# Routing from the residual's own rows: norm weights into the router's rows, norms into the logits

## The chip, the cores and the metric

One Trainium2 chip, of which the program uses one core. The metric is the device time of one launch in microseconds (us). The kernel before took 1364.86 us, the median of three runs (1364.3, 1364.86 and 1366.51 us).

## The reference

The reference is a decoder trunk of two layers on 256 tokens of width 1024, in float32. Layer 0 is a Conformer convolution beside cross-attention to a memory, then a dense SwiGLU. Layer 1 is a sliding-window attention beside cross-attention, then a mixture of eight experts of width 3584, of which each token takes two. What the change touches is the way from the end of layer 1's attention to the experts:

```
h  = h + swa_mixer(rms_norm(h, sw_attn_norm_g), ...)    # ends with concat([o, m]) @ w_out
hn = rms_norm(h, sw_ffn_norm_g)                         # h * rsqrt(mean(h*h) + eps) * g
logits = hn @ router                                    # 256 x 8
top_v, top_i = top_k(logits, 2); top_w = softmax(top_v)
h = h + sum_e gate_e * (silu(hn @ we_gate[e]) * (hn @ we_up[e])) @ we_down[e]
```

The logits are a sum over the channels of h, the norm's weight g and the router's row, times one number for each token, the root of the mean square.

## The kernel before

The kernel is written for a planner that places each engine's instructions in the order in which a timeline of its own finds them ready, earlier lines of the program first among the ready; it sets the semaphores itself. Each engine then runs its list in order, and so does SP, which issues nearly all loads. Inside the experts' loop TensorE's order is the written one (`manual_schedule`, L1026). A tile that is laid on bytes of an older tile waits until the older tile's last reader is done (`reuse_waits="tile"`).

Layer 1's attention writes its queries, transposed, into `q1T` (six blocks of 128 channels by 256 tokens, 1 KB a partition each, L582), the memory's queries into `mq1T` and the keys into `kTs`. The scores (L251) read them. The output projection (`project_out`, L308) goes over two halves n of the output's channels. In each half two accumulators, one for each 128 tokens t, take 24 products of 128x512 each (each float32 weight is split into a high and a low part, `mm3`). Then `add_residual` (L300) adds the accumulator to h, and takes the sum of squares for the norm; after the second half `token_rstd` gives rs2[t], the norm of each token.

The second part of the function opens new pools in the place of the first part's. `gain` (L673) is the norm's weight g, copied to all 128 partitions by one load of 512 KB (L674) on SP, and scaled by GpSimd (L675). After it SP issues the first 19 units of the experts' weights (L725), most of them 896 KB or 1 MB, each into a slot that the layers before leave free: two of the slots are those of layer 1's normed input, eight those of split weights, two those of the projection's input. `hn` (L756) is h times rs2 times `gain`, on VectorE. TensorE transposes hn block by block (L766), the copies go to `xT` (L767), and 16 matmuls against the router's rows (L770), each on 32 columns of the array, give partial logits `plt`. A copy (`lt`, L773) and four small matmuls (L776) add them up with tokens on partitions, and L778 copies the logits `lg`. From there a chain of small VectorE instructions finds the two best experts, counts the places with matmuls by triangular ones (L796 to L800), clears the accumulators `po` and `py` (L831, L833), and builds the selection matrices `Pm` of the first expert (L896). `gather` (L901) multiplies blocks of hn by Pm (32 matmuls, L909), which gives the first expert's tokens `xe`. Then the loop over 32 rounds (eight experts by four blocks of 896) begins: `gate_up` (L926), the same for a busy expert's further tokens (`gate_up_over`, L934, in four of the experts here), `down` (L982). After each round SP fetches the units of a later one into the slots that TensorE has read (`fetch`, L1062).

The small norm weights come in as rows through `param_rows` (L118, L368), are transposed at L401 and scaled at L403 to L406. In the new pools, `one` holds `lg`, `hn` and the small tiles, `mwk` the selection matrices, and `rt` holds `gain`, `router`, `xT` and `lt`. `wk`, `big` and `big1` are pools of the first part.

Of the kernel before, what the change touches and what calls it, by code (L numbers as in the profile page):

```python
# [7 lines left out]
F32 = mybir.dt.float32  # L8
# [5 lines left out]
OP = mybir.AluOpType  # L14
# [3 lines left out]
P = 128  # L18
S = 256
D = 1024  # L20
KD = D // P
# [3 lines left out]
HD = 64  # L25
FF = 2816
NE = 8
# [20 lines left out]
def hybrid_kernel(  # L48
# [7 lines left out]
    act, dve, pool, pe, sp = nc.scalar, nc.vector, nc.gpsimd, nc.tensor, nc.sync  # L56

    consts = ctx.enter_context(tc.tile_pool(name="consts", bufs=1))
# [44 lines left out]
    h = consts.tile([P, 2, D], F32, name="h")  # L103
# [3 lines left out]
    ident = consts.tile([P, P], F32, name="ident")  # L107
# [8 lines left out]
    offs = {}  # L116
# [16 lines left out]
    n0 = param_rows(rows0, (("cvg", cv_attn_norm_g, D), ("bglu", cv_b_glu, 2 * CH)), 0, first)  # L133
    for dst, src in first:
        sp.dma_start(dst, src)
    cols = consts.tile([P, P], F32, name="cols")
# [30 lines left out]
    with ExitStack() as ph:  # L167
# [5 lines left out]
        def bank(tag, name):  # L173

            if tag in ("mm", "tp"):
                return psb.tile([P, 512], F32, name=name, tag=tag)
            return psx[-1].tile([P, 512], F32, name=name, tag=tag,
                                bufs=dict(sc=2, cv=1, o=1, acc=4, so=1)[tag])
# [64 lines left out]
        big1 = None  # L243
# [56 lines left out]
        def add_residual(ps, t, n, ssum):  # L300
            hs = h[:, t, n * 512:(n + 1) * 512]
            dve.tensor_tensor(hs, ps, hs, op=OP.add)
            if n == 0:
                first_sum(ssum, t, hs, junk_tile())
            else:
                return token_rstd(ssum, t, hs, junk_tile())

        def project_out(unit, cT, order):  # L308

            ssum = new_sums()  # L310
            for n in range(2):
                acc = [bank("mm", f"wo{t}") for t in range(2)]
                w = []
                for i, t in ((0, 0), (0, 1), (1, 0), (1, 1)) if n == 0 else ((0, 0), (1, 0), (0, 1), (1, 1)):
                    if len(w) == i:
                        w.append(unit(n, i))
                    for j in range(4):
                        mm3(acc[t], [c[:, order[4 * i + j], t * P:(t + 1) * P] for c in cT],
                            [c[:, j, :] for c in w[i]], i == 0 and j == 0, i == 1 and j == 3)
                rs = [add_residual(acc[t], t, n, ssum) for t in range(2)]  # L320
            return rs


# [23 lines left out]
        eye4 = consts.tile([P, 32], F32, name="eye4")  # L347
# [15 lines left out]
        small = []  # L363
        for q in range(GT):
# [4 lines left out]
                                ("lnb", cv_ln_b, CH), ("hmk", mem_k_norm_g, HD), ("hmq0", cv_memq_norm_g, HD),  # L369
                                ("ffg", cv_ffn_norm_g, D), ("swg", sw_attn_norm_g, D),  # L370
                                ("hsq", sw_q_norm_g, HD), ("hsk", sw_k_norm_g, HD),
                                ("hmq1", sw_memq_norm_g, HD)), n0, small)
        for i in range(1, 3):
            for o in (0, CH):
                for dst, src in small[:5]:
# [25 lines left out]
        pe.transpose(pc[:, :n1 - n0], rows1[:n1 - n0, :], ident[:n1 - n0, :n1 - n0])  # L401
        dve.tensor_copy(cols[:, n0:n1], pc[:, :n1 - n0])
        for name, n, f in (("memg", KD, 32.0), ("ffg", KD, 32.0), ("swg", KD, 32.0),  # L403
                           ("hmk", 1, 8.0), ("hsk", 1, 8.0)):
            c = cols[:, offs[name]:offs[name] + n]
            dve.tensor_scalar_mul(c, c, f)  # L406

# [3 lines left out]
        router0 = consts.tile([P, KD, NE], F32, name="router0")  # L411
# [43 lines left out]
        for c in range(NCT):  # L455
# [8 lines left out]
            for g in range(GT):  # L464
                for q in range(4):
                    pe.matmul(pcv[q * 32:(q + 1) * 32, :], T[:, g, q, :], sh[q][:, 4 * g:4 * g + S],
                              start=(g == 0), stop=(g == GT - 1), tile_position=(0, q * 32))
# [104 lines left out]
        c1 = pair_tile("d")  # L572
# [79 lines left out]
                part(1, 1, 0, 3)  # L652
            return halves(t)

        rs2 = project_out(unit1, c1, wo_order)

# [2 lines left out]
    with ExitStack() as ph:  # L661
# [84 lines left out]
                           channel_multiplier=-1)  # L746
        onesb = one.tile([P, P], BF16, name="onesb")
        pool.memset(onesb, 1.0)
        router = rt.tile([P, KD, 32], F32, name="router")
        pool.memset(router, 0.0)  # L750
        pool.tensor_copy(router[:, :, 0:NE], router0)


        hn = one.tile([P, 2, D], F32, name="hn")
        for t in range(2):
            dve.scalar_tensor_tensor(hn[:, t, :], h[:, t, :], rs2[t][:, 0:1], gain, op0=OP.mult, op1=OP.mult)  # L756


        xT = rt.tile([P, KD, S], F32, name="xT")
        plt = bank("plt")[:, :S]  # L760
        for kk in range(KD // 2):
            b = prt.tile([P, 512], F32, name="rtb", tag="gu").rearrange("p (a n) -> p a n", a=2)
            for t in range(2):
                for a in range(2):
                    k = 2 * kk + a
                    pe.transpose(b[:, a, t * P:(t + 1) * P], hn[:, t, k * P:(k + 1) * P], ident)  # L766
            (act.copy if kk % 2 else dve.tensor_copy)(xT[:, 2 * kk:2 * kk + 2, :], b)  # L767
            for k in range(2 * kk, 2 * kk + 2):
                q = k % 4
                pe.matmul(plt[q * 32:(q + 1) * 32, :], router[:, k, :], xT[:, k, :], start=(k < 4), stop=(k >= 4),  # L770
                          tile_position=(0, q * 32))
        lt = rt.tile([P, S], F32, name="lt")
        act.copy(lt, plt)  # L773
        pl = bank("pl")
        for t in range(2):
            pe.matmul(pl[:, t * NE:(t + 1) * NE], lt[:, t * P:(t + 1) * P], eye4[:, 0:NE], start=True, stop=True)  # L776
        lg = one.tile([P, 2, NE], F32, name="lg")
        dve.tensor_copy(lg, pl[:, :2 * NE].rearrange("p (t e) -> p t e", t=2))  # L778
        mx = one.tile([P, 2, 8], F32, name="mx")
        ix = one.tile([P, 2, 8], U32, name="ix")  # L780
        ixf = one.tile([P, 2, 2], F32, name="ixf")
# [47 lines left out]
        py = [fixed(f"py{n}") for n in range(2)]  # L829

        dve.memset(po, 0.0)  # L831
        for n in range(2):
            dve.memset(py[n], 0.0)  # L833

        def gates():

# [53 lines left out]
        def places(e):  # L890

            pos = posm if e == 0 else posm2
            Pm = [wk.tile([P, 2, P], F32, name=f"Pm{n}", tag=f"Pm{n}", bufs=1) for n in range(2)]
            for n in range(2):
                for t in range(2):
                    dve.tensor_scalar(Pm[n][:, t, :], rows2[n], pos[:, t, e:e + 1], None, op0=OP.is_equal)  # L896
            return Pm
# [3 lines left out]
        def gather(e, Pm):  # L901

            xe = wk.tile([P, KD, SL], F32, name="xe", tag="xe")
            for kk in range(2):
                b = bank("ga")[:, :4 * SL].rearrange("p (k n) -> p k n", k=4)
                for a in range(4):
                    k = kk * 4 + a
                    for t in range(2):
                        pe.matmul(b[:, a, :], hn[:, t, k * P:(k + 1) * P], Pm[0][:, t, :SL], start=(t == 0),  # L909
                                  stop=(t == 1))  # L910
                (act.copy if kk else dve.tensor_copy)(xe[:, kk * 4:kk * 4 + 4, :], b)
            b = bank("pmt")
            for n in range(2):
                for t in range(2):
                    pe.transpose(b[:, n * S + t * P:n * S + (t + 1) * P], Pm[n][:, t, :], ident)
            PT = wk.tile([P, 2, S], F32R, name="PT", tag="PT")
            act.copy(PT, b.rearrange("p (n s) -> p n s", n=2))
            return xe, PT
# [106 lines left out]

        with tc.manual_schedule(engines={mybir.EngineType.PE}):  # L1026
            xe = {0: gather(0, places(0))}
            turns_of()
            gates()
            permuted(G2, G)  # L1030
            prev = None
            ys = None
            flag = None
            for i in range(len(rounds) + 1):
                last_round = i == len(rounds)
                if not last_round:
                    e, p = rounds[i]
                    wgu = [ahead.pop(0) for _ in range(8)]
                    if p == NR - 1 and e + 1 < NE:
                        Pm = places(e + 1)  # L1040
                    gate_up(xe[e][0], wgu, range(4))
                if prev is not None:
                    wd = [ahead.pop(0) for _ in range(4)]
                    hT, hTo = hidden_T(*prev[2:])
                if ys is not None:
                    scatter(*ys)
                    ys = None
                if not last_round:
                    if p == NR - 1 and e + 1 < NE:
                        xe[e + 1] = gather(e + 1, Pm)  # L1050
                    over_parts((e, xe[e][0], wgu, range(4)), None)
                    gate_up(xe[e][0], wgu, range(4, KD))
                    hx = hidden()
                over_parts(None if last_round else (e, xe[e][0], wgu, range(4, KD)),
                           None if prev is None else (prev[0], prev[1], hTo, wd))
                if prev is not None:
                    down(prev[1], hT, wd)
                    if prev[1] == NR - 1:
                        ys = (prev[0], outputs(), xe[prev[0]][1])
                if not last_round:  # L1060
                    prev = (e, p, hx, hidden_over())
                    fetch(8 + 4 * (i > 0))  # L1062
            scatter(*ys)
# [107 lines left out]
```

## Time and profile before

| | |
|---|---|
| median of three runs | 1364.86 us |
| the profiled execution's own time | 1362.78 us |
| its span, first to last instruction | 1361.1 us |
| TensorE matmul busy | 1286.2 us (94%) |
| VectorE, ScalarE, GpSimd busy | 387.5, 298.7, 70.7 us |
| mean granted TensorE clock | 0.980 of full speed |
| bytes moved | 420.87 MB, mean 309 GB/s |

The busy times are sums over the whole span; a matmul that waits in the array counts as busy, so 94% doesn't say that TensorE is what limits. The layers before the experts take the first 489 us, the experts the rest. A time in the rows below is counted from the first instruction.

### The profile page before, as it was taken

Reading aid. Unit: us, or ns where it says so; the run is one execution under the profiler, and the core shown is the slowest. Engines: PE = TensorE matmul, PEld = TensorE weight load, DVE = VectorE, ACT = ScalarE, POOL = GpSimd, SP = SyncE. Lnnn points to the kernel's source line nnn. Section 1 sums busy time; section 2 is a strip of 40 time slices with the busy share of each in tenths; the row PEclk is TensorE's granted clock in tenths of the full one; section 3 lists DMA queues with packets and bytes.
Section 4 is the critical chain, followed back from the end, with each engine's and each line's share of the span. In section 5 each row is a group of like instructions: output and inputs, shape, how many; then the busy total and the mean of one; then the engine's idle time right before and its main releaser. Section 6 shows DMA issues by size and latency. Waiting matters only on the chain. (4 is left out here: it accounts for less than half of the span.)

```text
span 1361.1 us, 19725 instructions
## 1 busy us (share of the span) xinstructions
PE 1286.2 (94%) x7908; PEld 720.4 (53%) x7908; DVE 387.5 (28%) x782; ACT 298.7 (22%) x575; POOL 70.7 (5%) x110
## 2 busy tenths in 40 slices
PE   6978799999898879999999999999999999999997
PEld 5844589999775643344454343444343454434443
DVE  5633465555466421012112111111110211100212
ACT  6333354444365300001111000011000111000111
POOL 4220200000031200000000000000000000000000
PEclk9989899999898988999999999999999999999999
DMA  9842145555472467989999999999999999999994
GB/s 291 291 132 72 63 149 198 184 184 184 124 223 83 191 230 299 363 336 394 413 409 409 409 412 404 409 410 412 409 409 404 411 409 408 412 411 409 403 411 199
DMA packets 137445, 420.87 MB, mean 309 GB/s; under 512 B 9658, under 2 KB 43256, under 8 KB 125048
## 3 DMA queue, kind: packets, MB, share of 16 engines
q1 hardware_dynamic: 133016, 414.39, 79.1%
q10 hardware_dynamic: 4320, 4.96, 1.1%
q8 instruction: 77, 1.26, 0.4%
q14 instruction: 32, 0.26, 0.1%
HBM read 417.37 MB, written 1.95 MB: 308 GB/s over the span
## 5 line engine op out<-in xcount | busy, mean ns | idle before, releaser
L926 PE MATMUL pa<-raw,xe 128*64 128x512 f32 x1024 | 269.8, 599 | 6.6 <-DVE hx L942 4.0
L926 PE MATMUL pb<-raw,xe 128*64 128x384 f32 x1024 | 213.2, 488 | 0.0
L982 PE MATMUL py<-raw,hT 128*64 128x512 f32 x896 | 199.3, 595 | 4.0 <-PEq L1023 1.6
L926 PEld LDWEIGHTS pb<-raw,xe 128*64 128x64 f32 x1024 | 81.1, 138 | 140.4 <-issue 140.4
L91 DVE TENSOR_TENSOR wlo<-raw,whi 128x1024 fp32r<-128x1024 f32 x108 | 131.9, 1260 | 80.8 <-ACT whi L90 80.8
L982 PEld LDWEIGHTS py<-raw,hT 128*64 128x64 f32 x896 | 67.5, 137 | 131.9 <-issue 121.4
L926 PEld LDWEIGHTS pa<-raw,xe 128*64 128x64 f32 x1024 | 77.5, 137 | 104.2 <-issue 70.0
L90 ACT CAST whi<-raw 128x1024 fp32r<-128x1024 f32 x112 | 111.5, 1046 | 54.5 <-issue 26.2
L934 PE MATMUL po<-raw,xe 128*32 128x512 f32 (+1 forms) x1024 | 116.3, 542 | 0.0
L975 DVE COPY hTo<-hto 128x224 f32<-128x224 f32 x32 | 12.5, 392 | 353.8 <-PE hto L973 353.8
L969 ACT COPY hT<-ht 128x448 f32<-128x448 f32 x32 | 17.1, 533 | 375.4 <-PE ht L967 375.4
L934 PEld LDWEIGHTS po<-raw,xe 128*32 128x32 f32 x1024 | 43.8, 109 | 55.2 <-issue 43.2
L992 PE MATMUL py<-raw,hTo 128*32 128x512 f32 x448 | 64.5, 594 | 3.3 <-PEq L1023 3.3
L942 DVE TENSOR_TENSOR hx<-s,pa 64x512 f32<-64x512 f32 x32 | 22.1, 690 | 152.6 <-ACT s L941 152.2
L958 DVE TENSOR_TENSOR hxo<-so,po 64x256 f32<-64x256 f32 x32 | 13.5, 423 | 156.8 <-ACT so L957 156.4
L941 ACT ACTIVATE s<-pa 64x512 f32<-64x512 f32 x32 | 18.9, 591 | 164.1 <-PE pa L926 163.8
L98 PE MATMUL fg<-xh,whi 128*128 128x256 f32 x176 | 50.2, 286 | 2.7 <-ACT fsg L557 2.5
L98 PE MATMUL fu<-xh,whi 128*128 128x256 f32 x176 | 50.1, 284 | 0.0
L99 PE MATMUL fu<-xh,wlo 128*128 128x256 f32 x176 | 50.1, 284 | 0.0
L100 PE MATMUL fg<-xl,whi 128*128 128x256 f32 x176 | 50.0, 284 | 0.0
L99 PE MATMUL fg<-xh,wlo 128*128 128x256 f32 x176 | 50.0, 284 | 0.0
L100 PE MATMUL fu<-xl,whi 128*128 128x256 f32 x176 | 49.9, 284 | 0.0
(297 smaller groups left out, 1620.4 us busy)
## 6 DMA issues: line engine op xcount, KB each, us to landing
raw<-in_sw_we_gate_dram SPq DMA_DIRECT2D x128, 896.0 KB
raw<-in_sw_we_up_dram SPq DMA_DIRECT2D x128, 896.0 KB
raw<-in_sw_we_down_dram SPq DMA_DIRECT2D x96, 1024.0 KB
raw<-in_sw_we_down_dram SPq DMA_DIRECT2D x32, 512.0 KB
raw<-in_cv_w_gate_dram SPq DMA_DIRECT2D x11, 1024.0 KB
raw<-in_cv_w_up_dram SPq DMA_DIRECT2D x11, 1024.0 KB
raw<-in_cv_w_down_dram SPq DMA_DIRECT2D x11, 1024.0 KB
raw<-in_cv_w_in_dram SPq DMA_DIRECT2D x7, 1024.0 KB
```

What stands on the lines that cost most here:

```text
L90: act.copy(hi[:, i:i + step], v[:, i:i + step])
L91: (low or dve).tensor_tensor(lo[:, i:i + step], v[:, i:i + step], hi[:, i:i + step].bitcast(F32), op=OP.subtract)
L98: pe.matmul(ps, ah, bh, start=first, stop=False)
L99: pe.matmul(ps, al, bh, start=False, stop=False)
L100: pe.matmul(ps, ah, bl, start=False, stop=last)
L926: pe.matmul(ps[half * HD:(half + 1) * HD, :c1 - c0], x, v[:, c0:c1], start=(k == 0), stop=(k == KD - 1), tile_position=(0, half * HD))
L934: pe.matmul(po[q * 32:(q + 1) * 32, :c1 - c0], x, v[:, k % 2, c0:c1], start=(k == 0), stop=(k == KD - 1), tile_position=(0, q * 32))
L941: act.activation(s[:HD, :], pa[:HD, :], AF.Silu)
L942: dve.tensor_tensor(hx[:HD, :], s[:HD, :], pa[HD:, :], op=OP.mult)
L969: act.copy(hT, b[:, :3 * P + HD])
L982: pe.matmul(py[n][n * HD:(n + 1) * HD, :], hT[:, o:o + HD], w[q // 2][:, q % 2, n * 512:(n + 1) * 512], start=(p == 0 and q == 0), stop=(p ...
L992: pe.matmul(py[n][r:r + 32, :], hTo[:, o:o + 32], w[q // 2][:, q % 2, n * 512:(n + 1) * 512], start=(i < 2), stop=(i >= NR * BLK - 2), til ...
```

## The change

The norm's weight joins the small rows (`mog`), so that it is there with channels on partitions, and is multiplied into the router's rows once, in `big1` (GpSimd). The router's transposes read h itself instead of hn. They are called through `route(n)` from `project_out`, after each half of the channels is added: the first half's four blocks after n = 0, the other four after n = 1. Their copies go into `q1T` (blocks 0 to 5) and `mq1T` (blocks 6 and 7), which the attention has read by then, the partial logits' copy into `kTs`; their PSUM tiles are of the attention's kinds (`tp`, `sc`). The logits are multiplied by rs2 where they were copied, and `lg` moves to `consts`. The two clears of `py` move behind the first gather. `gain` and `hn` stay as they are, for the gather.

```diff
-        def project_out(unit, cT, order):
+        def project_out(unit, cT, order, after=None):
...
                 rs = [add_residual(acc[t], t, n, ssum) for t in range(2)]
+                if after:
+                    after(n)
...
-                                ("hmq1", sw_memq_norm_g, HD)), n0, small)
+                                ("hmq1", sw_memq_norm_g, HD), ("mog", sw_ffn_norm_g, D)), n0, small)
...
-                           ("hmk", 1, 8.0), ("hsk", 1, 8.0)):
+                           ("mog", KD, 32.0), ("hmk", 1, 8.0), ("hsk", 1, 8.0)):
...
-        rs2 = project_out(unit1, c1, wo_order)
+        router = big1.tile([P, KD, 32], F32, name="router")
+        pool.memset(router, 0.0)
+        g0 = offs["mog"]
+        pool.tensor_tensor(router[:, :, 0:NE], router0, cols[:, g0:g0 + KD, None].to_broadcast([P, KD, NE]), op=OP.mult)
+        plt = bank("sc", "plt")[:, :S]
+
+        def route(n):
+            for kk in range(2 * n, 2 * n + 2):
+                b = bank("tp", "rtb").rearrange("p (a n) -> p a n", a=2)
+                xT = q1T[:, 2 * kk:2 * kk + 2, :] if kk < 3 else mq1T
+                for t in range(2):
+                    for a in range(2):
+                        k = 2 * kk + a
+                        pe.transpose(b[:, a, t * P:(t + 1) * P], h[:, t, k * P:(k + 1) * P], ident)
+                (act.copy if kk % 2 else dve.tensor_copy)(xT, b)
+                for a in range(2):
+                    k = 2 * kk + a
+                    q = k % 4
+                    pe.matmul(plt[q * 32:(q + 1) * 32, :], router[:, k, :], xT[:, a, :], start=(k < 4),
+                              stop=(k >= 4), tile_position=(0, q * 32))
+
+        rs2 = project_out(unit1, c1, wo_order, route)
+        lt = kTs[:, 0, :]
+        act.copy(lt, plt)
+        pl = bank("sc", "pl")
+        lg = consts.tile([P, 2, NE], F32, name="lg")
+        for t in range(2):
+            pe.matmul(pl[:, t * NE:(t + 1) * NE], lt[:, t * P:(t + 1) * P], eye4[:, 0:NE], start=True, stop=True)
+        for t in range(2):
+            dve.tensor_scalar_mul(lg[:, t, :], pl[:, t * NE:(t + 1) * NE], rs2[t][:, 0:1])
...
-        router = rt.tile([P, KD, 32], F32, name="router")
-        pool.memset(router, 0.0)
-        pool.tensor_copy(router[:, :, 0:NE], router0)
...
-        xT = rt.tile([P, KD, S], F32, name="xT")
-        plt = bank("plt")[:, :S]
-        for kk in range(KD // 2):
-            ...                                  # the same loop over kk, on hn
-        lt = rt.tile([P, S], F32, name="lt")
-        act.copy(lt, plt)
-        pl = bank("pl")
-        ...
-        dve.tensor_copy(lg, pl[:, :2 * NE].rearrange("p (t e) -> p t e", t=2))
...
         dve.memset(po, 0.0)
-        for n in range(2):
-            dve.memset(py[n], 0.0)
...
             xe = {0: gather(0, places(0))}
+            for n in range(2):
+                dve.memset(py[n], 0.0)
             turns_of()
```

## Rows read from the trace of the kernel before

**Rows 1.** Stretches: length, busy (count) by engine, granted clock, DMA share, GB/s.
```profile
480.00:485.00 5.00, 2.42 (x11) 2.46 (x12) 4.58 (x30) 0.00 (x0) 0.00 (x0) 0.50 1.00 412
485.00:490.00 5.00, 5.00 (x34) 4.08 (x35) 3.48 (x15) 0.97 (x2) 0.00 (x0) 0.83 0.04 16
500.00:520.00 20.00, 15.98 (x86) 5.61 (x84) 2.37 (x6) 2.99 (x5) 0.00 (x0) 0.83 0.81 312
580.00:620.00 40.00, 39.85 (x260) 18.35 (x258) 4.58 (x13) 3.80 (x8) 0.00 (x0) 1.00 0.87 334
620.00:660.00 40.00, 38.87 (x203) 15.88 (x201) 9.14 (x19) 4.92 (x11) 0.00 (x0) 1.00 1.02 411
1200.00:1300.00 100.00, 98.73 (x600) 40.80 (x592) 15.21 (x34) 10.43 (x23) 0.00 (x0) 1.00 1.02 408
```

**Rows 2.** Waits of TensorE's weight loads, 488 to 640 us: total, times, longest.
```profile
PEld pa L926 <- DMA raw<-in_sw_we_down_dram: 0.2, 1, 0.2
```

**Rows 3.** Timeline of TensorE, 443 to 489 us: start, length, what, count, wait.
```profile
444.46 1.03 PE L251 MATMUL sc<-kTs,q1T 64*128 64x256 f32 x4
...
468.55 0.39 PE L100 MATMUL wo<-wlo,dh 128*128 128x512 f32 x1
472.38 3.16 PE L766 MATMUL rtb<-ident,hn 128*128 128x128 f32 x16 [3.44 <-DVE hn L756]
475.47 1.52 PE L770 MATMUL plt<-xT,router 128*32 128x256 f32 x16
477.49 0.61 PE L776 MATMUL pl<-eye,lt 128*128 128x8 f32 x4 [0.50 <-ACT lt L773]
...
482.58 5.74 PE L909 MATMUL ga<-Pm,hn 128*128 128x96 f32 x32 [2.58 <-DVE Pm L896]
...
488.68 0.65 PE L926 MATMUL pa<-raw,xe 128*64 128x512 f32 x2
```

**Rows 4.** The same of VectorE.
```profile
467.77 0.95 DVE L161 CUSTOM_DVE_ANT_0 junk<-h,ssum 128x512 bf16<-128x512 f32 x1
...
468.98 0.69 DVE L302 TENSOR_TENSOR h<-wo,h 128x512 f32<-128x512 f32 x1 [0.25 <-PE wo L100]
...
471.04 2.48 DVE L756 SCALAR_TENSOR_TENSOR hn<-h,rt,gain 128x1024 f32<-128x1024 f32 x2
...
475.15 0.69 DVE L767 COPY xT<-rtb 128x512 f32<-128x512 f32 x1 [0.16 <-PE rtb L766]
478.14 0.17 DVE L778 COPY lg<-pl 128x16 f32<-128x16 f32 x1 [2.30 <-PE pl L776]
...
481.28 1.02 DVE L833 MEMSET py<- 128x512 f32 x2
482.22 0.74 DVE L896 TENSOR_SCALAR Pm<-rows,posm 128x128 f32<-128x128 f32 x4
```

**Rows 5.** Timeline of SP, which issues the loads, 458 to 500 us.
```profile
458.91 0.37 SPq L684 DMA_DIRECT2D raw<-in_sw_we_up_dram  x1
459.37 0.42 SPq L684 DMA_DIRECT2D raw<-in_sw_we_gate_dram  x1
459.89 0.42 SPq L674 DMA_DIRECT2D gain<-in_sw_ffn_norm_g_dram  x1
463.97 0.37 SPq L684 DMA_DIRECT2D raw<-in_sw_we_up_dram  x1
...
469.68 27.45 SPq L684 DMA_DIRECT2D raw<-in_sw_we_down_dram  x3
```

**Rows 6.** Timeline of GpSimd from 467 us.
```profile
467.13 2.80 POOL L675 TENSOR_SCALAR gain<-gain 128x1024 f32<-128x1024 f32 x1 [13.39 <-DMA gain<-in_sw_ffn_norm_g_dram]
```

**Rows 7.** Stretches of half a microsecond where the loads run out.
```profile
484.50:485.00 0.50, 0.50 (x4) 0.50 (x4) 0.39 (x4) 0.00 (x0) 0.00 (x0) 0.50 0.91 377
485.00:485.50 0.50, 0.50 (x4) 0.50 (x4) 0.43 (x3) 0.00 (x0) 0.00 (x0) 0.50 0.25 98
```

**Rows 8.** Timeline of SP, one of the early loads.
```profile
22.15 0.40 SPq L77 DMA_DIRECT2D raw<-in_cv_w_in_dram  x1
```

More of the change, by code (lines that the diff above doesn't have):

```diff
@@ L756, in hybrid_kernel @@
             dve.scalar_tensor_tensor(hn[:, t, :], h[:, t, :], rs2[t][:, 0:1], gain, op0=OP.mult, op1=OP.mult)
-        xT = rt.tile([P, KD, S], F32, name="xT")
-        plt = bank("plt")[:, :S]
-        for kk in range(KD // 2):
[L762 to L771, printed above, removed]
-        lt = rt.tile([P, S], F32, name="lt")
-        act.copy(lt, plt)
-        pl = bank("pl")
-        for t in range(2):
-            pe.matmul(pl[:, t * NE:(t + 1) * NE], lt[:, t * P:(t + 1) * P], eye4[:, 0:NE], start=True, stop=True)
-        lg = one.tile([P, 2, NE], F32, name="lg")
-        dve.tensor_copy(lg, pl[:, :2 * NE].rearrange("p (t e) -> p t e", t=2))
         mx = one.tile([P, 2, 8], F32, name="mx")
```

## The prediction

> **What bounds the kernel now.** I read the table of stretches first. From 620 us to the end the loads are busy all the time, at 408 to 411 GB/s [rows 1]: the experts' weights set the pace there, and no work of an engine shortens that part. It can only begin earlier or later. In front of it lies a stretch, 485 to 620 us, in which the loads stand still or run at part speed (16, 312, 334 GB/s) and TensorE is busy [rows 1]: the slots are full, and a new unit is fetched only when TensorE has read an old one. Through this stretch TensorE waits for a load once, for 0.2 us [rows 2]. So the loads follow TensorE's first round, and whatever moves the first expert matmul (`pa`, 488.68 us [rows 3]) moves the whole rest by as much. The question is when that matmul starts.
>
> Before it, the timelines of TensorE and VectorE show one serial chain [rows 3, 4]: the output projection's last matmul (468.55 us), the last addition to h (468.98), hn (471.04, 2.48 us), sixteen transposes (472.38), the router's matmuls (475.47), the small ones (477.49), the logits (478.14), the choice of experts, the clear of `py` (1.02 us), `Pm` (482.22), the gather (482.58, 5.74 us), `pa`. The change cuts into this chain. But the gather multiplies hn, and hn needs `gain`, the norm's weight on all partitions. Its load, issued at 459.89 us, and its scaling on GpSimd (467.13 to 469.93) end just before hn starts and so are hidden today [rows 5, 6].
>
> **What the change takes from the chain.** The transposes read h, so hn leaves the path to the logits (2.48 us). Half of the transposes and router matmuls (3.16/2 + 1.52/2 = 2.3 us [rows 3]) go before the last addition to h. The part that comes before the projection's last matmul lengthens it, by 0 to 2.3 us; TensorE has no idle time there, the other part falls into the wait for the addition: 1 us. Of the second half a serial rest stays: the last transposes (about 0.7 with their latency), a copy (about 0.6), eight matmuls (0.8), `lt`, the small matmuls (0.6), two scalings in place of one copy (0.2 more): about 4 us after an addition that ends at 469.7 + 1 us. The logits come at 474.6 instead of 478.2 us, 3.6 us earlier, and the selection matrices 1 us more, since `py` is cleared behind the gather. If nothing else were due, the gather would start 4 to 5 us earlier.
>
> **What the change puts in its place.** The copies of the transposes go into `q1T`. I lay out the pools by the tile sizes in the code, in bytes of a partition, from the start of `big`, which is also the start of `one`. First part: `mkT` and `mv` 4096, `wk` about 14,400 (two each of 2048, 1024, 2056 and 2048), `dist` 1024, `kTs` and `vsw` 2048 each. So `q1T` lies at 23,616 to 29,760. Second part: `one` about 12,540 (hn alone 8192), less 64 for `lg`; `mwk` 12,288 (`Pm` 2048, `xe` 6144, `PT` 4096); then `gain`, at about 24,770 to 28,870. It lies on `q1T` blocks 1 to 5. Before the change `q1T` was last read by the attention's last scores at 444.46 us [rows 3], and the load of `gain` was held by nothing when SP came to it [rows 5]. With the change `q1T` is written and read again by the second half of the routing: blocks 4 and 5 are transposed only after the last addition to h, and the router's matmuls read them near 472.5 us. The load of `gain` may not be issued before.
>
> That alone would cost little. But SP's list is made by readiness, and every slot of the 19 units is free before: the last two by 469.68 us (the row of three issues holds two at once, and the third, a unit of the loop, that ends at 497.13) [rows 5]. So `gain` goes behind all of them. The queue is full by then: it moves 412 GB/s until 485 us and runs out by 485.25 [rows 1, 7]. The bytes are the same in another order, so the queue ends at the same time, and `gain` is now its last piece instead of its third. Loads of SP come in the order of issue: `gain` took 7.24 us from issue to use [rows 5, 6], where it and the two units of 896 KB before it, 2.36 MB, need 5.8 us at 409 GB/s. Had it shared the bandwidth with the units issued behind it, it would have come later.
>
> The sum on the new path:
> - queue ends 485.25 us [rows 7]. Bounds 484.5 to 487: the first issue of this batch waits for the projection, which may be up to 2.3 us longer, or not longer at all.
> - last byte to GpSimd: of the 7.24 us 1.4 are not transfer, for start and landing together; a running queue needs no start. 0 to 1.4, taken 0.8.
> - scaling on GpSimd 2.80 us [rows 6], the same instruction. Bounds 1.85 to 2.80: VectorE's sum of squares (0.95 us [rows 4]) ran beside it and may have held it up. I take 2.80, its own row.
> - hn 2.48 us [rows 4]; both halves are needed, since the gather's second matmul reads the second.
> - hn done: 485.25 + 0.8 + 2.8 + 2.5 = 491.35 us. The gather's first matmul runs in the shadow of the second half of hn (0.2 us).
> - gather to `pa`: 488.68 - 482.58 = 6.1 us [rows 3]. The granted clock was 0.50 (1.2 GHz) when this gather began, after a stretch with TensorE nearly idle [rows 1], and TensorE is idle before the new one too, so 6.1 stands.
> - `pa` at 491.15 + 6.1 = 497.25 us, 8.6 us later than before.
>
> On the Trainium skill: "SBUF — State Buffer", "Who interferes with whom", says that VectorE instructions with two SBUF inputs and GpSimd instructions that read SBUF block each other. VectorE would be idle beside the new scaling, so by that rule the sum would be up to 0.95 us smaller, 7.6. The row can't tell, because the sum of squares, which began second, also grew.
>
> All else hides under this wait. The earlier logits, the two clears and the first expert's selection are done by 480 us while the gather waits until 491. The one extra small load sits among SP's early issues, where the next takes 0.4 us [rows 8]; 0 to 0.5 us, taken as nothing, with TensorE fed by earlier units there. The extra rows in one transpose and one more scaling of eight columns are under 0.2 us on VectorE. The product with the router's rows is a GpSimd instruction with the whole attention as its cover. None of these can bring a gain of its own, as the gather doesn't wait for them.
>
> Sum: 1362.78 + 8.6 = 1371.4 us for the profiled execution's own time (its span 1361.1 and 1.7 around it). It lies 2.1 us under the median of the runs, 1364.86, so the forecast on that footing is 1373.5 us. Ends of the sum: every lower bound gives 484.5 + 0 + 1.85 + 2.48 = 488.8, 2.55 us under the sum's 491.35, so 6 us later than before; every upper one 487 + 1.4 + 2.8 + 2.5 = 493.7, 11 us later. The likeliest case has 1371 to 1376.
>
> **Rivals.**
> 1. *The norm's tile isn't held* (faster). My layout may be off, and `gain` may lie clear of `q1T`; the mechanism is then the shortened chain alone. It would have to be off by more than 4 KB on one side, which the sizes don't give. The logits come 3.6 us earlier and `Pm` 1.0 more, less some 0.4 us of hn that still stands in VectorE's list before them: 4.2 us, 1360.7 us. Chance 0.10. It decides if the load is issued before about 465 us.
> 2. *`gain` gets ahead of some units on SP.* Its line is written before theirs, so where the planner's timeline holds units back longer than I think, it goes first, and they queue behind it. Each unit it passes (896 KB to 1 MB at 409 GB/s) saves 2.2 to 2.6 us of its landing. Two units: 3.6 us later than before, 1368.5. If it passes all that are still to move, it is issued at 472.5 with an empty queue and takes some 3 us (1.3 of transfer at that rate, and the 1.4 above); hn is then done at 480.8, the gather starts 2 us earlier, and 1363 us comes out. Chance 0.10, half of it within 0.2% of before. By the Trainium skill's "DMA: Bandwidth & Descriptors", "Anatomy of one DMA — SWDGE (gpsimd) path", a lone load takes about 2.0 us + bytes / 436 GB/s, 3.2 us here; the 7.24 us of the trace contain the queue and don't test it.
> 3. *hn is placed too early in VectorE's list.* If the planner believes that `gain` lands soon, hn stands before the logits, and the choice of experts waits behind it on the same engine: from the logits to the gather 482.58 - 478.14 = 4.4 us [rows 3, 4], less 1.0 for `py`. 3.4 us more, 1376.9 us. For it: the list is made by the planner's time of a load, which doesn't see the queue. Against it: even a load of 3 us and the scaling of 2.8 put hn after the logits' chain. Chance 0.08.
>
> **Chances and range.** The forecast 0.70, the rivals as given, 0.02 for the rest. A measurement of this kernel tells a change from none at about 0.2%, 2.7 us. Faster: 0.10. Within 0.2%: 0.06 (half of rival 2 and a little of the rest). Slower: 0.84. The range 1366 to 1378 us holds the forecast's own, rival 3 and most of rival 2, and leaves out rival 1.
>
> **What would show it.** In the profile after: SP issues the norm's load after the two last projection-fed units, past 472 us; GpSimd's scaling starts at about 486, waiting for that load; hn runs at 489 to 491; the logits are there by 476 and TensorE idle from then to 491; the loads stand still from 486 to over 500; `pa` starts near 497, and the full-rate stretch later by the same 8 to 9 us. It is wrong if the scaling starts before 475 us, if the gather waits for `Pm` rather than hn, or if `pa` moves and the end doesn't follow.

## The result and the profile after

The changed kernel takes 1372.8 us (median of 6 runs, 1370.1 to 1375.3), the kernel before beside it 1364.8; the ratio is 1.0052, 95% interval 1.0038 to 1.0067. That is slower by 8.0 us by the medians and by 7.1 us by the ratio, where 1373.5 us was forecast, within 1366 to 1378. The profiled execution took 1375.27 us (span 1373.6), the longest of its runs.

Before stages are compared, one caution: the two profiled executions already differ by more than the change does to the work up to there. The last addition to h begins at 471.91 us instead of 468.98 [rows 4], and over all kernels of this study, with or without the change, that time lies anywhere from 468.98 to 474.95 us. So below I count times from that addition ("after the addition").

SP's timeline after (start, length, line, what) answers [rows 5]:

```profile
461.96 0.42 SPq L718 DMA_DIRECT2D raw<-in_sw_we_gate_dram  x1
466.89 0.37 SPq L718 DMA_DIRECT2D raw<-in_sw_we_up_dram  x1
...
472.61 1.15 SPq L718 DMA_DIRECT2D raw<-in_sw_we_down_dram  x2
475.43 0.33 SPq L708 DMA_DIRECT2D gain<-in_sw_ffn_norm_g_dram  x1
511.62 0.33 SPq L718 DMA_DIRECT2D raw<-in_sw_we_down_dram  x1
```

The norm's load, third of its batch before, is now the last: it is issued behind the two units of `down`, 1.67 us after SP was done with them, and nothing follows it for 36 us. GpSimd's and VectorE's timelines (as [rows 6] and [rows 4]):

```profile
491.02 2.82 POOL L709 TENSOR_SCALAR gain<-gain 128x1024 f32<-128x1024 f32 x1 [12.04 <-DMA gain<-in_sw_ffn_norm_g_dram]
```

```profile
471.91 0.69 DVE L302 TENSOR_TENSOR h<-wo,h 128x512 f32<-128x512 f32 x1 [0.46 <-PE wo L100]
...
477.29 0.36 DVE L689 TENSOR_SCALAR lg<-pl,rt 128x8 f32<-128x8 f32 x2 [2.82 <-PE pl L687]
...
480.44 0.74 DVE L903 TENSOR_SCALAR Pm<-rows,posm 128x128 f32<-128x128 f32 x4
...
493.87 2.48 DVE L787 SCALAR_TENSOR_TENSOR hn<-h,rt,gain 128x1024 f32<-128x1024 f32 x2 [7.16 <-POOL gain L709]
```

The choice of experts is indeed quicker: logits 5.38 us after the addition (9.16 before), `Pm` 8.53 us (13.24 before). From 486.7 us on VectorE has nothing to do: `hn` starts only 21.96 us after the addition, since it waits for GpSimd's scaling, which waits for the load (12.04 us, in brackets above). TensorE's timeline (as [rows 3]) shows the end of that wait:

```profile
476.57 0.61 PE L687 MATMUL pl<-eye,kTs 128*128 128x8 f32 x4 [0.47 <-ACT kTs L683]
...
495.21 0.74 PE L916 MATMUL ga<-Pm,hn 128*128 128x96 f32 x2 [15.90 <-DVE hn L787]
496.40 6.72 PE L916 MATMUL ga<-Pm,hn 128*128 128x96 f32 x30 [0.45 <-DVE hn L787]
...
503.50 1.08 PE L933 MATMUL pa<-raw,xe 128*64 128x512 f32 x4
```

`pa` starts 31.59 us after the addition, against 19.70 before: 11.89 us later. The stretches (as [rows 1]) show the loads standing still until the first round frees slots, and full rate again past 640 instead of 620 us:

```profile
485.00:490.00 5.00, 0.00 (x0) 0.00 (x0) 1.54 (x7) 0.00 (x0) 0.00 (x0) 0.50 0.78 321
490.00:505.00 15.00, 9.34 (x44) 8.06 (x46) 3.91 (x7) 1.77 (x3) 2.82 (x1) 0.57 0.00 1
...
620.00:640.00 20.00, 19.01 (x112) 7.57 (x108) 2.76 (x7) 2.24 (x5) 0.00 (x0) 1.00 0.98 387
640.00:1000.00 360.00, 356.20 (x2070) 155.00 (x2070) 56.63 (x131) 36.37 (x80) 0.00 (x0) 1.00 1.02 409
```

From the addition to the end of the span the kernel before needs 892.1 us (1361.1 - 468.98), the changed one 901.7: 9.6 us more, not 11.9. So 2.3 us are given back behind `pa`. They are in the first round: from `pa` to the matmuls `ht` below it is 32.26 us before and 29.99 after, and from there to the end 840.2 and 840.1. ScalarE's part of the round and TensorE's wait in it, first before, then after:

```profile
508.43 1.28 ACT L956 ACT_TABLE_LOAD   x1 [19.05 <-PE po L934]
509.72 0.48 ACT L956 ACTIVATE so<-po 64x384 f32<-64x384 f32 x1
```

```profile
512.22 1.97 PE L926 MATMUL pa<-raw,xe 128*64 128x512 f32 x4 [4.02 <-DVE hx L942]
...
520.94 0.62 PE L966 MATMUL ht<-ident,hx 128*128 128x128 f32 x3
```

```profile
504.26 1.28 ACT L963 ACT_TABLE_LOAD   x1
523.13 0.48 ACT L963 ACTIVATE so<-po 64x384 f32<-64x384 f32 x1 [17.58 <-PE po L941]
```

```profile
525.63 1.08 PE L933 MATMUL pa<-raw,xe 128*64 128x512 f32 x4 [2.60 <-DVE hx L949]
...
533.49 0.62 PE L973 MATMUL ht<-ident,hx 128*128 128x128 f32 x3
```

Before, ScalarE loads a table (1.28 us) only when `po` is there, and TensorE waits 4.02 us for what follows. After, the same table load runs at 504.26 without a wait, long before `po`: the wait is 2.60 us, 1.42 less. And the matmuls of the next part, up to `ht`, take 7.86 us instead of 8.72: before, the granted clock is down to 0.50 (1.2 GHz) when they begin and stays there for 5.2 us of them (512.2 to 517.4); after, it falls only behind their start and is low for 3.4 (526.9 to 530.3), read from stretches of 1 us. 1.42 + 0.86 = 2.28 us. This is read from the two profiles; no run takes the two parts apart.

### The profile page after: what moved, and what is told of

It is laid out like the page before. It is cut to its first block, busy times and chain, and to the rows that moved or that the text cites. A ratio compares the mean times of both kernels' runs of the same rounds, so it can differ in the third digit from the quotient of the medians.

```text
span 1373.6 us, 19732 instructions
## 1 busy us (share of the span) xinstructions
PE 1288.9 (94%) x7908; PEld 722.2 (53%) x7908; DVE 387.3 (28%) x784; ACT 298.7 (22%) x575; POOL 69.8 (5%) x110
```

## The experiments

Each kernel was run with the one before on the same chip. The table has, in us after the addition: the first use of `gain` (before: ahead of the addition), the end of hn, the start of `pa`; then, as "tail", by how much the time from the addition to the end of the span differs from the 892.1 us of before; and the measured ratio to the kernel before with its interval.

| kernel | gain used | hn done | pa | tail | ratio |
|---|---|---|---|---|---|
| before | (-1.85) | 4.54 | 19.70 | 0 | 1 |
| changed | 19.11 | 24.44 | 31.59 | +9.6 | 1.0052 (1.0038 to 1.0067) |
| e2, hold in before | 18.48 | 23.80 | 40.07 | +20.3 | 1.0149 (1.0128 to 1.0171) |
| e3, ScalarE's queue | 11.32 | 18.69 | 25.30 | +3.6 | 1.0020 (1.0008 to 1.0033) |
| e6, no hold | 18.81 | 24.26 | 31.72 | +10.0 | 1.0071 (1.0053 to 1.0088) |
| e9, ahead of two | 13.97 | 19.42 | 25.94 | +3.9 | 1.0020 (1.0006 to 1.0034) |
| e7, ahead of eight | 9.34 | 15.02 | 21.99 | 0.0 | 0.9995 (0.9985 to 1.0004) |
| e4, no scaling | 19.09 | 21.57 | 28.49 | +6.6 | 1.0036 (1.0022 to 1.0049) |
| e8, no gain load | none | 6.69 | 15.49 | -6.5 | 0.9953 (0.9940 to 0.9966) |
| e10, and warm | none | 6.69 | 15.46 | -6.7 | 0.9955 (0.9940 to 0.9970) |

In every kernel with the change the tail moved by 2.0 to 2.5 us less than `pa`; in e2, which has only the hold, by 0.1. So the end follows `pa` one to one, and the 2.3 us are a gain of the changed program that hardly depends on how late it is.

**The hold alone, in the kernel before (e2).**

```diff
         rs2 = project_out(unit1, c1, wo_order)
+        dve.tensor_copy(q1T[:, 4, 0:1], h[:, 1, 512:513])
```

> The kernel before with one tiny copy added: after the output projection VectorE writes one element of a row into q1T (a tile that nothing reads later), so that the bytes under the norm's load are busy until the last addition to h. Nothing of the change itself is in it. My theory (the load of gain, held by a late user of q1T, falls behind all 19 units on SP's list, and the batch's queue is what it costs): gain's issue past 469.7 us instead of 459.89, its first use at 486 to 491 instead of 467.13, and since here the transposes and the whole choice of experts stand behind hn, pa at 507 to 511.5 us (use + 2.8 + 2.5 + 9.1 + 6.1) instead of 488.7: 18 to 23 us later, about 2 given back later, 1380 to 1386 us. Rival (the tile's hold costs nothing, and what was slower in the changed kernel is the longer projection and the moved transposes): 1364 to 1367 us.

```profile
474.04 0.38 SPq L675 DMA_DIRECT2D gain<-in_sw_ffn_norm_g_dram  x1
```

```profile
490.67 2.81 POOL L676 TENSOR_SCALAR gain<-gain 128x1024 f32<-128x1024 f32 x1 [13.67 <-DMA gain<-in_sw_ffn_norm_g_dram]
```

1386.3 us, by the ratio 20.3 us over before. One late write of one element into the bytes under `gain` moves its load from 459.89 to 474.04, behind all units (issue order as in the changed kernel), and its use to 18.48 us after the addition. So the hold alone is enough to put the load last, without anything else of the change. The price is twice as high because the transposes and the choice stand behind hn here: from the end of hn to `pa` it is 16.27 us, against 7.15 in the changed kernel. The expected range was 1380 to 1386 us; the time lies 0.3 us above it.

**The hold taken away (e6), and gain ahead of two (e9) or eight (e7) units.**

```diff
-        gain = rt.tile([P, D], F32, name="gain")
+        gain = one.tile([P, D], F32, name="gain")
...
-        hn = one.tile([P, 2, D], F32, name="hn")
-        for t in range(2):
-            dve.scalar_tensor_tensor(hn[:, t, :], h[:, t, :], rs2[t][:, 0:1], gain, op0=OP.mult, op1=OP.mult)
+        hn = gain, one.tile([P, D], F32, name="hn")
+        for t in (1, 0):
+            dve.scalar_tensor_tensor(hn[t], h[:, t, :], rs2[t][:, 0:1], gain, op0=OP.mult, op1=OP.mult)
...                                              # the gather reads hn[t] for hn[:, t]
```

and in e9 besides (in e7 with 11 for 17, so that eight units go behind it, as many as in the kernel before), where `loaded` is the issue of gain's load:

```diff
-        fetch(len(RING))
+        fetch(17)
+        with tc.issue_after(loaded.ins):
+            fetch(len(RING) - 17)
```

> The changed kernel with gain laid on other bytes (first tile of the pool of hn, and one half of hn is then written over it), so that no late reader holds its load; in SP's list it still stands behind all 19 units, as the order now comes out without the hold. My theory (place in the queue is the price, not the wait for q1T's readers): gain's issue at 473 to 474 instead of 475.43, but the use still at the queue's end, 489 to 491 us, 1370 to 1374 us as the changed kernel. Rival (the hold is the price): the use comes earlier by the 2 to 2.5 us of the earlier issue or more, 1368 to 1370.5. In either case the first step of my prediction, that the hold by q1T puts the load last, would not be the only cause, as it is last without it.

> The kernel of the run e6 with one edge more: the last two of the 19 units (1 MB each) are to be issued behind gain. Nothing else moves. My theory (each unit that gain passes saves its transfer, 1,048,576 bytes at 409 GB/s = 2.56 us): use of gain 5.1 us earlier than in e6, about 485 to 486, hn done at 490.5 to 491.5, pa and the end 5 us earlier than e6: 1366 to 1369.5 us. Rival A (transfers of one list share the bandwidth, so that gain ahead of two units gains half or less): 1370 to 1372. Rival B (the hold and not the queue): as e6.

> The kernel of the run e6 with an edge that puts eight of the 19 units behind gain on SP's list (in e9 it was two). The price of the edge: these eight, some of which were issued from 461 us on, now all wait until the projection has freed its slots, past 472. My theory (each unit passed saves its transfer until another wait ends later): use of gain 4 to 8 us after the last addition to h (18.8 in e6, 14.0 in e9), then VectorE's list is the bound, since hn stands behind most of the choice of experts there: hn 12.5 to 15 us after the addition, pa 21.5 to 24 us after it, against 25.9 in e9 and 31.6 in the changed kernel; the late units cost nothing, since the first round reads them later: 1363.5 to 1366.5 us. Rival (the eight late units are missed by the first round): TensorE waits for loads between 490 and 520 us, 1367 to 1370.

SP's timeline of e6, then of e9:

```profile
473.79 1.12 SPq L718 DMA_DIRECT2D raw<-in_sw_we_down_dram  x2
474.95 0.68 SPq L708 DMA_DIRECT2D gain<-in_sw_ffn_norm_g_dram  x1
```

```profile
474.28 0.41 SPq L718 DMA_DIRECT2D raw<-in_sw_we_up_dram  x1
474.74 0.46 SPq L708 DMA_DIRECT2D gain<-in_sw_ffn_norm_g_dram  x1
475.25 33.18 SPq L718 DMA_DIRECT2D raw<-in_sw_we_down_dram  x3
```

In e6 the load follows the last unit at once (0.04 us; 1.67 us in the changed kernel), so no tile holds it: its new bytes are by the layout those of `mkT` and `mv`, which TensorE reads for the last time near 429 us. Yet it is used as late as in the changed kernel: 18.81 against 19.11 us. The ratios' intervals overlap. So the wait for q1T's readers costs some 0.3 us by itself, and the place in the queue the rest. It also shows that the load is last in SP's list without the hold: that it takes my hold to put it there is wrong, something else does it as well.

In e9, where only the order of three loads differs from e6, the use comes 4.84 us earlier; 2 MB at 409 GB/s are 5.1 us, so the two units behind the load take at most 0.3 us from it. With the gather, of which less ran at 1.2 GHz (6.52 us from hn to `pa` instead of 7.46), that is 5.8 of the 6.1 us by which the tail is shorter than in e6. The time, 1368.2 us, lies within its range, and rivals A and B are out. In e7 the use is 9.34 us after the addition, not the 4 to 8 expected; hn starts 0.27 us after the scaling's end, at its place in VectorE's list:

```profile
470.41 0.41 SPq L718 DMA_DIRECT2D raw<-in_sw_we_up_dram  x1
470.88 0.46 SPq L708 DMA_DIRECT2D gain<-in_sw_ffn_norm_g_dram  x1
471.38 0.56 SPq L718 DMA_DIRECT2D raw<-in_sw_we_up_dram  x1
```

```profile
479.52 2.82 POOL L709 TENSOR_SCALAR gain<-gain 128x1024 f32<-128x1024 f32 x1 [2.27 <-DMA gain<-in_sw_ffn_norm_g_dram]
```

```profile
482.61 1.28 DVE L789 SCALAR_TENSOR_TENSOR hn<-h,rt,gain 128x1024 f32<-128x1024 f32 x1
```

The load took 8.64 us from issue to use, more than the 7.24 us of [rows 5, 6]. In both kernels it goes behind two units into a queue that had run empty; before, the row is

```profile
459.00:459.50 0.50, 0.50 (x4) 0.33 (x2) 0.00 (x0) 0.00 (x0) 0.00 (x0) 1.00 0.00 0
```

What differs is what comes behind the load: there the next unit is issued 4.1 us after it [rows 5], here 0.5 us, and more follow. That these take the 1.4 us from it is not shown; but [rows 5, 6], with nothing close behind the load, say little on whether it shares the bandwidth with later units. From hn on the sum holds (`pa` at 21.99 us, 21.5 to 24 expected), and the eight late units cost nothing: the tail is that of before, and the time, 1364.4 us, within the range.

**Gain on another queue (e3).**

```diff
-        sp.dma_start(gain, bass.AP(...
+        act.dma_start(gain, bass.AP(...
```

> The changed kernel with the load of gain issued by ScalarE instead of SP; the data hold by q1T stays (issue about 476.5 us, after the router's last matmuls and ScalarE's copy of the logits' sums). My theory (the price is the place behind the units in one list of SP): the load doesn't stand behind the 19 units, is used 3 to 5 us after its issue, at 479.5 to 481.5 us instead of 491.0, scaled by 484.3; hn then starts when VectorE's list comes to it, at 486.7 instead of 493.87, so pa comes 7 us earlier: 1364 to 1367 us. Rival A (all outstanding loads share the bandwidth whatever list they come from, so it lands with the backlog): use near 489 to 491, 1370 to 1373 us. Rival B (the price is the hold until the routing is done, not the queue): no change, 1372.8.

The instructions of `gain` in e3 (count, least/median/greatest ns, first and last start), then VectorE's timeline:

```profile
L708 ACTq DMA_DIRECT2D gain<-in_sw_ffn_norm_g_dram x1: 368/368/368, 473.3 to 473.3; - x1
L709 POOL TENSOR_SCALAR gain<-gain x1: 2817/2817/2817, 480.4 to 480.4; 128x1024 f32<-128x1024 f32 x1
```

```profile
480.38 1.05 DVE L882 TENSOR_TENSOR rk<-rk 128x8 f32<-128x8 f32 x1
...
482.41 0.78 DVE L889 CAST turnf<-turn 128x8 f32<-128x8 uint32 x1
```

Issued by ScalarE at 473.3 us, held by q1T as in the changed kernel, the load is used 7.0 us later (3 to 5 expected), while SP's backlog still has 6 us to run: the loads move 385 GB/s from 485 to 486 us and 98 in the microsecond after. (The profile's timeline names an instruction of VectorE as the end of GpSimd's wait; by the code the scaling needs the load alone.) So rival A, by which it lands with the backlog, and rival B both fall. The time, 1367.6 us, is 0.6 us above my range. hn started 16.22 us after the addition; VectorE's list was done with what stands before it at 14.8 us in the changed kernel. The difference is in the two rows: beside GpSimd's scaling they took 1.05 and 0.78 us, where they take 0.17 each in the changed kernel.

**Without the scaling (e4).**

```diff
-        pool.tensor_scalar(gain, gain, 32.0, None, op0=OP.mult)
...
+            pool.tensor_scalar(r32[:, t:t + 1], rs2[t], 32.0, None, op0=OP.mult)
```

> The changed kernel without GpSimd's scaling of gain: the factor 32 is put into the reciprocal root (two instructions of one column each, early on GpSimd), so that hn reads gain as it lands. My theory (on the new path queue, scaling and hn stand one behind the other, and the scaling counts with its whole 2.82 us): hn starts when the load lands, 19.1 us after the last addition to h instead of 22.0; 2.8 us less than the changed kernel, 1368.5 to 1371 us. Rival (VectorE's list or a later landing sets hn's start, so the scaling is partly hidden): 1371.5 to 1373.5.

```profile
494.04 2.48 DVE L788 SCALAR_TENSOR_TENSOR hn<-h,r,gain 128x1024 f32<-128x1024 f32 x2 [4.28 <-DMA gain<-in_sw_ffn_norm_g_dram]
```

hn now waits for the load itself and starts 19.09 us after the addition instead of 21.96: 2.87 us. The tail is 2.9 us shorter than the changed kernel's. By the ratios it is 2.2 us, with intervals that overlap; the time, 1370.9 us, lies in my range and not in the rival's, but it is the profile that shows the scaling to count in full.

**Without the load (e8), and TensorE kept at work (e10).**

```diff
-        act.copy(lt, plt)
+        lt_done = act.copy(lt, plt)
...                                              # gain, its load and its scaling are left out
-            dve.scalar_tensor_tensor(hn[:, t, :], h[:, t, :], rs2[t][:, 0:1], gain, op0=OP.mult, op1=OP.mult)
+            with tc.issue_after(lt_done.ins):
+                act.mul(hn[:, t, :], h[:, t, :], rs2[t][:, 0:1])
...
-                (act.copy if kk else dve.tensor_copy)(xe[:, kk * 4:kk * 4 + 4, :], b)
+                g4 = cols[:, g0 + 4 * kk:g0 + 4 * kk + 4, None].to_broadcast([P, 4, SL])
+                dve.tensor_tensor(xe[:, kk * 4:kk * 4 + 4, :], b, g4, op=OP.mult)
```

and in e10 six `pe.matmul(warm, ident, ident)`, three ahead of and three behind the count of places.

> The changed kernel without the tile gain, its load and its scaling: hn is h times the reciprocal root alone, on ScalarE behind the copy of the logits' sums, and the norm's weights are multiplied in when the gathered rows are copied out of PSUM (VectorE, both halves; before, ScalarE had one). My theory (the shortened chain of the change is real and was only covered by the wait for gain): the gather waits for Pm, starting 8.9 us after the last addition to h where it was 13.6 before the change, and pa follows 6.1 to 7.1 us behind, 15 to 16 us after the addition, against 19.7 before; another 2.3 us between pa and the second gather, which every kernel with the change has shown (ScalarE's table load off the first round's wait, and less half-speed time behind it): 5 to 7 us under the kernel before, 1358.5 to 1360.5 us. Rival (the shortening is eaten up, by hn on ScalarE, by the second copy on VectorE, or by the gather's clock): 1362 to 1365.

> The kernel of the run e8 with six matmuls of 128x128 by 128 columns on TensorE, whose result nobody reads: three between the logits and the count of places, three between that and the gather. They fill two waits. My theory (the granted clock comes back some time after TensorE is at work again, so that an earlier start brings the gather under the full clock sooner): the clock rises 1.5 to 3 us earlier within the gather, which gets 0.8 to 2 us shorter: 1356.5 to 1359.5 us, 1 to 2 under e8. Rival (the small pauses between them keep the clock down, and the six only delay the count of places): as e8 or up to 0.7 us more.

Timelines of e8, VectorE and TensorE:

```profile
479.33 0.74 DVE L900 TENSOR_SCALAR Pm<-rows,posm 128x128 f32<-128x128 f32 x4
```

```profile
479.69 6.24 PE L913 MATMUL ga<-Pm,hn 128*128 128x96 f32 x32 [1.50 <-DVE Pm L900]
486.29 1.08 PE L931 MATMUL pa<-raw,xe 128*64 128x512 f32 x4
```

1358.2 us: faster than both kernels, 6.4 us under before by the ratio, and 0.3 us under my range. `pa` comes 4.21 us earlier after the addition than before the change, which is the 4.2 us of my first rival, and 2.3 us are given back as in all kernels with the change. The shortened chain was there all along; one load hid it and took 12 us more.

e10 gained nothing (1359.2 us, the intervals nearly the same): not the 1 to 2 us under e8 that I expected, as its rival had it. Its stretches (columns as in [rows 1]), then those of e8:

```profile
479.00:480.00 1.00, 1.00 (x6) 0.89 (x5) 0.89 (x8) 0.00 (x0) 0.00 (x0) 0.50 1.01 409
484.00:485.00 1.00, 1.00 (x7) 1.00 (x6) 0.97 (x6) 0.00 (x0) 0.00 (x0) 0.50 0.93 385
485.00:486.00 1.00, 1.00 (x9) 1.00 (x9) 0.35 (x3) 0.00 (x0) 0.00 (x0) 0.87 1.08 451
```

```profile
484.00:485.00 1.00, 1.00 (x8) 1.00 (x6) 0.86 (x5) 0.00 (x0) 0.00 (x0) 0.58 1.01 410
485.00:486.00 1.00, 1.00 (x12) 1.00 (x11) 0.90 (x5) 0.00 (x0) 0.00 (x0) 1.00 0.98 410
```

TensorE was at work from 479 us on, and yet the clock rose near 485.3 us, 14.0 us after the addition, as in e8 (484.8, also 14.0). The six matmuls delayed nothing, and the gather took 6.20 us instead of 6.24.

## Why the prediction was right

The mechanism was right in each link that sets the time: the load behind all units (seen, and by e9 worth 2.4 us for each megabyte it passes), the scaling in full (e4), hn behind it, the gather behind hn (`Pm` was ready 14 us earlier, so it bound nothing), and the end with `pa` (e2). The reason given for the first link was incomplete: the hold by `q1T` is enough to put the load last (e2), but the load is last without it too (e6). That the forecast didn't need its own reason is luck. Rival 1 would have been right about its price (e8) but not about its condition: e6 lays gain clear of q1T and is no faster. Rival 2's price per unit, 2.2 to 2.6 us, is e9's 2.42. The 3.2 us that the prediction has there from the Trainium skill ("DMA: Bandwidth & Descriptors", "Anatomy of one DMA — SWDGE (gpsimd) path") stay untested: no run has this load alone in the queues, and the section's figure is for loads that GpSimd issues, where SP issues this one. Rival 3 did not occur: hn stood behind the whole choice of experts in VectorE's list.

The sizes, by the terms of the sum. It had `pa` 28.27 us after the addition (497.25 - 468.98); it came at 31.59.

- **The queue's end and the landing** were mis-sized, by 2.0 us together: the first use of `gain` was put at 486.05, 17.07 us after the addition, and measured at 19.11. "The bytes are the same in another order, so the queue ends at the same time" was a wrong step. The rows of half a microsecond around the gap and the end:

```profile
468.00:468.50 0.50, 0.50 (x4) 0.42 (x3) 0.00 (x0) 0.00 (x0) 0.00 (x0) 1.00 0.73 72
468.50:469.00 0.50, 0.50 (x4) 0.39 (x3) 0.00 (x0) 0.00 (x0) 0.00 (x0) 1.00 0.65 194
...
488.50:489.00 0.50, 0.00 (x0) 0.00 (x0) 0.00 (x0) 0.00 (x0) 0.00 (x0) 0.50 0.58 229
489.00:489.50 0.50, 0.00 (x0) 0.00 (x0) 0.00 (x0) 0.00 (x0) 0.00 (x0) 0.50 0.22 90
```

With gain gone from its third place, the queue ran short from 467.5 to 469.5, until the projection freed the next slots: 199 GB/s on average instead of 409, 1.0 us of transfers lost, and they come back at the end. Where the rate has fallen to 90 GB/s, as to 98 in [rows 7], the queue counts as ended: 489.25 us, 17.3 us after the addition and 1.1 later than the sum had it. The other 1.0 us is the landing: GpSimd starts at 491.02, 1.8 us behind that. I had taken 0.8 us for it.

- **The gather** was taken at 5.9 us from the end of hn to `pa` (6.1 less the shadow of 0.2); it was 7.15. Before, the clock rose at 486.7 us, 4.1 us after the gather's first matmul; after, at 503.0, 7.8 us after it, so that nearly all of the gather ran at 1.2 GHz. The rows, before and after:

```profile
486.00:487.00 1.00, 1.00 (x8) 1.00 (x8) 0.87 (x3) 0.00 (x0) 0.00 (x0) 0.66 0.06 25
```

```profile
502.00:503.00 1.00, 1.00 (x7) 1.00 (x7) 0.00 (x0) 0.00 (x0) 0.00 (x0) 0.50 0.00 0
503.00:504.00 1.00, 1.00 (x9) 0.55 (x9) 0.61 (x4) 0.79 (x2) 0.00 (x0) 0.99 0.00 0
```

"So 6.1 stands" went by the clock at the gather's start; no row gave when it would rise. TensorE had been idle for 15.9 us here and for 2.6 before, but the idle time alone doesn't order the kernels: it was 12.1 us in e9 and 1.5 in e8, and the clock rose 4.8 and 5.1 us after the gather's first matmul. What sets the moment stays open.

- **The scaling** took 2.82 us. By the rule that the prediction cites from the Trainium skill, "SBUF — State Buffer", "Who interferes with whom" (VectorE instructions with two SBUF inputs and GpSimd instructions that read SBUF contend), it put up to 0.95 us less with VectorE idle. The trace shows no such gain: GpSimd's scaling took 2.80 us beside VectorE's sum of squares and 2.82 alone. It was VectorE's instruction that paid: 0.95 us beside the scaling [rows 4], 0.75 for the next sum of squares, at 470.16 us.

- **The projection** got 0.34 us longer, not 1 (from the first unit issued in it to the addition: 10.07 us before and in e2, 10.41 after and in e3). A time counted from the addition leaves this out.

- **The logits** came 3.8 us earlier after the addition and `Pm` 4.7. With the 0.34 us of the projection that is 3.4 and 4.4, where 3.6 and 4.6 were predicted: the projection was 0.7 us shorter than taken, and the serial rest behind the addition as much longer (4.7 us from its end to the logits, not 4).

- **Given back** 2.3 us, which no step foresaw. Together: predicted 8.6, plus 3.3 for queue, landing and gather, less 2.3, is 9.6 us from the addition on, what the profiled executions show; the projection's 0.3 come on top. The runs show 8.0 by the medians and 7.1 by the ratio, 2 to 3 us less than the two profiles, and no trace says why. The profiled execution itself took 1375.27 us where 1371.4 was predicted for it, and 2.9 of these 3.9 us are the later addition. So that the forecast, 1373.5, came within 1 us of the median, 1372.8, is luck in good part: errors of several microseconds that cancel.

## What to carry to other kernels

A tile laid on another's bytes inherits that tile's last reader; when a change gives an old tile a new late use, look up what lies on it and what loads wait. A small load that a serial step needs should not stand behind bulk loads on one list: here each megabyte ahead of it cost 2.4 us (e9), and not needing it (weights folded into a copy that is made anyway, e8) beat every way of placing it that was tried. Count from a common event behind the drift of the early stages, or the difference of two profiles is read wrongly by several microseconds (2.9 here).

## What was not expected, and what stays open

Beside GpSimd's scaling single instructions of VectorE stretch, not the scaling: 0.17 to 1.05 us and 0.17 to 0.78 in e3, and in e7 one of 8 columns took 0.75 us (0.23 in the changed kernel) and ended with the scaling. The rule of the Trainium skill named above ("SBUF — State Buffer", "Who interferes with whom") fits the first of them, which has two inputs in SBUF. But the same instruction kept its 0.17 us beside the scaling of e7, as did other two-input ones (0.16 to 0.17 us), so the rule alone doesn't say which stretch. That was not tested.

The time of the last addition to h differs by up to 6 us between executions whose work up to there is the same but for 0.34 us. Where it is late, the profiled execution is long for its kernel: 4.5 us above the median of the runs in e4 (474.95), 2.0 below it before (468.98). So a good part of the runs' spread seems to come from there; its cause was not looked for. Nor is it settled what places the load last in SP's list when no tile holds it (e6).
